# Sums of squares of a two-layer decoder trunk: four column groups of TensorE in place of two, with four-row transposes behind the copies

## The chip, the cores and the metric

The kernel runs on one core of one Trainium2 chip. The metric is the device time of one execution in microseconds (us); lower is better. Three runs of the kernel before gave 801.45, 801.98 and 802.34 us, so its median is 801.98 us.

## The reference

The reference is a decoder trunk of two layers on 528 tokens (16 meta tokens and 512 others) of width 1024. Each layer normalizes its input, projects it, lets a pooling mixer and a latent attention run side by side, and adds their gated merge to the residual stream:

```python
def rmsnorm(x, gain):
    inv = lax.rsqrt(jnp.mean(xf * xf, axis=-1, keepdims=True) + NORM_EPS)
    return xf * inv * gain
...
for l in range(DEPTH):                       # DEPTH = 2
    h = rmsnorm(h_res, norm_gain[l])         # over 1024 features
    proj = h @ w_in[l]                       # u, z, c_q (768), c_kv (256), k_rope, z_mla, gates
    y_pool = (pool_mix(u_pool, ...) * silu(z_pool)) @ pool_w_up[l]
    o_mla = mla(c_q, c_kv, k_rope, ...)      # begins with rmsnorm of c_q and of c_kv
    y_mla = (o_mla * silu(z_mla)) @ mla_w_up[l]
    merged = sigmoid(g_pool) * y_pool + sigmoid(g_mla) * y_mla
    h_res = h_res + merged @ w_out[l]
```

The change concerns two of the norms: that of the layer's input x (a sum of squares over 1024 features per token) and that of c_kv (over 256 features per token).

## The kernel before

Activations are kept transposed: features on the 128 partitions, the 528 tokens along the free axis, so that x is eight tiles of 128 by 528. Every large product is split in three fp32r matmuls (`mm3`, lines 190 to 192: high part of the weights with the high and the low part of the activations, and low part of the weights with the high part). A token axis that is too long for one matmul is done in two segments, `FULL = [(0, 264), (264, 528)]`.

All large products stand in one list (`register`), and `stream()` is a generator that issues them one by one. ScalarE (ACT) converts the weights that arrive by DMA to their high part (line 185), VectorE (DVE) makes the low part (line 186). `go()` issues a layer's other work, and `fill_now(ns)` lets the stream issue about so many nanoseconds of matmuls between two steps of that other work, so that TensorE (PE) has something to do while the other engines work. That is only the order in which the program names the instructions: a scheduler then fixes the order on each engine, after a simulated timeline of its own. Each engine carries out its own instructions strictly in that order, and an instruction that waits holds up all behind it on its engine.

Because the features lie on the partitions, a sum of squares over features is a matmul with a matrix of ones. `norm_sums` (lines 355 to 399) does this once in each layer, for both norms:

1. Eight tiles of squares of x (`xsq`) and two of c_kv (`csq`), each in two segments of 264 tokens, are multiplied by `ones[:, 0:32]` at line 363: 20 matmuls in fp32, each of which the hardware carries out as two passes. A matmul of 32 output rows uses one of four column groups of the array, chosen by `tile_position=(0, r_)`; its result lands in the 32 PSUM partitions of that group. Segment 0 of x uses group 0 and segment 1 uses group 64; c_kv uses groups 32 and 96.
2. Two ACT copies (line 370) bring rows 0 to 63 of `sums` out of PSUM: row 0 holds the sums of x, row 32 those of c_kv. A DVE copy (line 371) repeats the 16 meta tokens eight times in `rep`.
3. Five PE transposes (lines 375 and 376) of 33 rows put the tokens on the partitions, and DVE works out the reciprocal roots (lines 381 to 383, `newton`, lines 391 to 393).
4. `rows` (lines 404 to 410) transposes the roots back into rows of `kinv`, and `spread` (lines 283 to 287) multiplies them by a selector so that every partition holds them: four matmuls at line 286, each followed by an ACT copy at line 287 to `rinv` (for x) or to a tile for c_kv. `ev_u` (line 491) and later evacuations multiply by these.

The other lines that the prediction names: line 346 to 351 make the split input and its squares, line 539 to 550 evacuate the c_q products (ACT copy, DVE remainder, ACT square, GpSimd sum), line 430 is a matmul for k_rope in eight 32-column pieces that uses all four column groups, and line 813 is the 128 by 128 transpose of attention.

PSUM tiles named mm come from a ring of four banks (`mmt`). A PE instruction that needs a bank waits until the last reader of that bank's previous tile has finished.

Of the kernel before, what the change touches and what calls it, by code (L numbers as in the profile page):

```python
# [9 lines left out]
F32 = mybir.dt.float32  # L10
# [3 lines left out]
AF = mybir.ActivationFunctionType  # L14
ALU = mybir.AluOpType
# [3 lines left out]
P = 128  # L19
DEPTH = 2  # L20
D = 1024
SEQ = 512
NM = 16
T = SEQ + NM
HALF = T // 2
# [46 lines left out]
def trunk(ctx, tc, xT, pos, win, wkr, wqb, wkb, wvb, wgr, wpu, wmu, wout, gains, const, yT):  # L72
    nc = tc.nc
    pe, act, dve, gp, sp = nc.tensor, nc.scalar, nc.vector, nc.gpsimd, nc.sync
# [5 lines left out]
    sm = ctx.enter_context(tc.tile_pool(name="sm", bufs=1))  # L80
# [5 lines left out]
    def nm(s):  # L86
        uid[0] += 1
        return f"{s}_{uid[0]}"

    def slot(tag, dt=F32, bufs=1, w=W):  # L90
        return sl.tile([P, w], dt, tag=tag, name=nm(tag), bufs=bufs)

    def tmp(w=W):
        return tp.tile([P, w], F32, tag="tmp", name=nm("tmp"), bufs=3)
# [4 lines left out]
    def mmt():  # L99
        return pp.tile([P, 512], F32, tag="mm", name=nm("mm"), bufs=4)  # L100

    def sct():
        return pp.tile([P, 512], F32, tag="S", name=nm("S"), bufs=3)
# [27 lines left out]
    ident = cst[:, C_ID:C_ID + P]  # L131
    ones = cp.tile([P, P], F32, name="ones")
# [141 lines left out]
    def fill_now(ns):  # L274
        end = clk[0] + ns
        while clk[0] < end and step():
            pass
# [5 lines left out]
    def spread(dst, i):  # L283
        for a, b in FULL:
            ps = mmt()[:, :b - a]
            pe.matmul(ps, sel[0:34, i:i + 1].to_broadcast([34, P]), kinv[:, a:b], start=True, stop=True)
            act.activation(dst[:, a:b], ps, AF.Copy)

    def behind(ins, other):
        tc.add_manual_dep(ins.ins, other.ins.name,  # L290
                          mybir.DependencyInfo(mybir.DependencyClass.Sync, mybir.DependencyReason.DATA))

    def newton(y, a, t):
        dve.tensor_single_scalar(y.bitcast(I32), a.bitcast(I32), 1, op=ALU.logical_shift_right)
        dve.tensor_scalar(y.bitcast(I32), y.bitcast(I32), -1.0, float(0x5F3759DF), op0=ALU.mult, op1=ALU.add)
        dve.tensor_scalar(a, a, -0.5, None, op0=ALU.mult)
        for _ in range(3):
            dve.tensor_mul(t, y, y)
            dve.tensor_mul(t, t, a)
            dve.scalar_tensor_tensor(out=y, in0=t, scalar=1.5, in1=y, op0=ALU.add, op1=ALU.mult)  # L300
# [20 lines left out]
    class Layer:  # L321
# [32 lines left out]

        def norm_sums(self):
            fill_now(2600)
            ps = [mmt(), mmt()]
            for t, r, start, stop in [(self.xsq[k], 0, k == 0, k == 7) for k in range(6)] + [
                    (self.csq[0], 32, True, False), (self.xsq[6], 0, False, False),
                    (self.xsq[7], 0, False, True), (self.csq[1], 32, False, True)]:  # L360
                for s, (a, b) in enumerate(FULL):
                    r_ = r + 64 * s
                    mm = pe.matmul(ps[s][r_:r_ + 32, :HALF], ones[:, 0:32], t[:, a:b], start=start, stop=stop,  # L363
                                   tile_position=(0, r_))
                    if t is not self.csq[1]:
                        behind(mm, self.csq_last)
            sums = tmp()
            rep = sm.tile([64, 8, NM], F32, tag="rep", name=nm("rep"))
            for s, (a, b) in enumerate(FULL):
                act.activation(sums[0:64, a:b], ps[s][64 * s:64 * s + 64, :HALF], AF.Copy)  # L370
            dve.tensor_copy(rep, sums[0:64, 0:NM].unsqueeze(1).to_broadcast([64, 8, NM]))
            fill_now(2600)
            ps = mmt()[:, 0:165].rearrange("p (j c) -> p j c", c=33)
            for j in range(4):
                pe.transpose(ps[:, j, :], sums[0:33, NM + P * j:NM + P * (j + 1)], ident[0:33, 0:33])
            pe.transpose(ps[:, 4, :], rep[0:33].rearrange("p a b -> p (a b)"), ident[0:33, 0:33])
            na = sm.tile([P, 2, 5], F32, tag="na2", name=nm("na2"))
            nt = sm.tile([P, 2, 5], F32, tag="nt2", name=nm("nt2"))
            self.ninv = ny = sm.tile([P, 2, 5], F32, tag="ny2", name=nm("ny2"))
            self.eps = sm.tile([P, 5], F32, tag="eps", name=nm("eps"))  # L380
            dve.tensor_scalar(na[:, 0, :], ps[:, :, 0], 1.0 / D, EPS, op0=ALU.mult, op1=ALU.add)
            dve.tensor_scalar(self.eps, na[:, 0, :], EPS, None, op0=ALU.mult)
            dve.scalar_tensor_tensor(out=na[:, 1, :], in0=ps[:, :, 32], scalar=1.0 / 256, in1=self.eps,
                                     op0=ALU.mult, op1=ALU.add)
            newton(ny, na, nt)
            w = tmp()
            gp.memset(w[:, 0:170], 0.0)
            v = w[:, 0:170].rearrange("p (j c) -> p j c", c=34)
            nv = ny.rearrange("p a j -> p j a")
            nh = sm.tile([P, 5, 2], F32R, tag="nh", name=nm("nh"))  # L390
            dve.tensor_copy(nh, nv)
            dve.tensor_copy(v[:, :, 0:33:32], nh.bitcast(F32))
            dve.tensor_sub(v[:, :, 1:34:32], nv, nh.bitcast(F32))
            fill_now(8200)
            self.rows(v, 34, kinv)
            self.inv, self.cinv = slot("rinv"), slot("cq9")
            fill_now(1300)
            spread(self.inv, 0)
            spread(self.cinv, 1)
            self.st = [sct(), sct()]  # L400
# [727 lines left out]
```

## Time and profile before

| | us |
|---|---|
| median of three runs | 801.98 |
| the profiled execution, its own time | 802.28 |
| its span, from the first to the last instruction | 800.5 |
| PE busy within the span | 792.9 |
| DVE busy | 527.4 |
| ACT busy | 416.9 |
| GpSimd (POOL) busy | 196.4 |
| median duration of one pass at line 363 | 0.386 |
| median duration of one copy at line 370 | 0.386 |

Times within the span are counted from its first instruction. Rows of the timeline give the start, the duration (of several merged rows, from the first start to the last end), the engine, the line, and in brackets how long the engine sat idle before it and what ended that. Matmuls are pipelined: rows overlap, and what a matmul costs is the distance from its start to the next start. PE counts each pass of an fp32 matmul as a row, so line 363 shows 40 rows for each layer.

### The profile page before, as it was taken

To read this page: it belongs to the slowest core of one execution; us is meant where nothing else is said; L and a number is where in the kernel's file an instruction comes from. 1 tells how busy PE (TensorE), PEld (TensorE's weight loads), DVE (VectorE), ACT (ScalarE), POOL (GpSimd) and SP (SyncE) were. 2 spreads that over 40 slices of the span, in tenths; PEclk is the share of its full clock that TensorE was granted. 3 is DMA by queue.
4 is the path that set the end of the run, shared out by engine and by line. 5 is a ranking of instruction groups with operands and counts; after the bars stand their busy time and mean duration, and the time that the engine had idled before them with its cause. 6 is when DMAs were issued, how large, how long until landed. Compare 5 with 4: busy or idle time off the path is not lost.

```text
span 800.5 us, 14638 instructions
## 1 busy us (share of the span) xinstructions
PE 792.9 (99%) x5339; PEld 714.0 (89%) x5339; DVE 527.4 (66%) x1140; ACT 416.9 (52%) x947; POOL 196.4 (25%) x266
## 2 busy tenths in 40 slices
PE   9999999999999999999999999999999999999998
PEld 8889999999999999999997997877788888887887
DVE  5568767437679887585354686665467889665942
ACT  7455645545556665543254456446455666654421
POOL 1024404103333322142000163022024333410600
PEclk9999999999999999999999999999999999999999
DMA  6223233424222222234642222334253322222372
GB/s 240 74 69 93 71 100 90 110 83 143 83 87 87 80 67 67 81 91 142 181 143 73 73 87 86 92 86 119 82 154 97 100 77 79 76 69 78 92 232 97
DMA packets 48872, 80.71 MB, mean 101 GB/s; under 512 B 5904, under 2 KB 14480, under 8 KB 48800
## 3 DMA queue, kind: packets, MB, share of 16 engines
q1 hardware_dynamic: 48656, 79.52, 33.5%
q8 instruction: 42, 0.69, 0.4%
q14 instruction: 30, 0.25, 0.1%
q10 hardware_dynamic: 144, 0.26, 0.1%
HBM read 73.40 MB, written 4.23 MB: 97 GB/s over the span
## 4 chain that ended last, share of the span: by engine, by line
PE 96%; DMA 2%; DVE 1%; ACT 1%; issue 0%; POOL 0%; POOLq 0%
PE mm L190 28%; PE mm L192 28%; PE mm L191 27%; PE mm L813 2%; PE S L191 2%; PE S L192 1%; PE S L190 1%; PE o L819 1%; PE o L818 1%; PE mm L363 1%; PE S L472 1%; DMA xb<-xT 1%; DMA bc<-kdr 1%; PE mm L430 0%; DMA rinv<-win 0%; PE mm L406 0%
## 5 line engine op out<-in xcount | busy, mean ns | idle before, releaser
L190 PE MATMUL mm<-hh,whi 128*128 128x264 f32 (+2 forms) x1096 | 346.0, 318 | 0.4 <-ACT racc L827 0.2
L191 PE MATMUL mm<-hl,whi 128*128 128x264 f32 (+2 forms) x1096 | 343.5, 314 | 0.0
L192 PE MATMUL mm<-hh,wlo 128*128 128x264 f32 (+2 forms) x1096 | 342.0, 315 | 0.0
L186 DVE TENSOR_TENSOR wlo<-raw,whi 128x512 fp32r<-128x512 f32 (+2 forms) x251 | 185.5, 743 | 118.1 <-ACT whi L185 110.8
L185 ACT ACTIVATE whi<-raw 128x512 fp32r<-128x512 f32 (+2 forms) x251 | 150.3, 602 | 186.2 <-PE mm L191 131.1
L190 PEld LDWEIGHTS mm<-hh,whi 128*128 128x128 f32 x1096 | 205.6, 188 | 13.8 <-ACT racc L827 0.5
L191 PEld LDWEIGHTS mm<-hl,whi 128*128 128x128 f32 x1096 | 206.2, 188 | 12.2 <-issue 0.4
L192 PEld LDWEIGHTS mm<-hh,wlo 128*128 128x128 f32 x1096 | 205.0, 188 | 12.7 <-issue 0.4
L719 POOL TENSOR_TENSOR tmp<-kp,bc 64x528 f32<-64x528 f32 x16 | 24.5, 1532 | 113.2 <-DMA bc<-kdr 77.9
L550 POOL TENSOR_TENSOR racc<-racc,tmp 128x264 f32<-128x264 f32 (+1 forms) x15 | 14.1, 942 | 143.1 <-ACT tmp L549 143.0
L791 POOL TENSOR_TENSOR pm<-pa,rs 128x16 f32<-128x16 f32 x32 | 11.6, 361 | 145.6 <-DVE rs L786 145.6
L901 POOL TENSOR_TENSOR tmp<-tmp,xb 128x264 f32<-128x264 f32 (+1 forms) x24 | 26.9, 1143 | 58.6 <-DVE tmp L899 33.0
L747 DVE CUSTOM_DVE_ANT_0 S<-S,maskw,nqs 128x272 f32<-128x272 f32 (+4 forms) x80 | 38.4, 498 | 1.6 <-PE S L192 1.2
L754 ACT ACTIVATE cq<-S,bia 128x400 f32<-128x400 f32 (+2 forms) x48 | 24.6, 516 | 21.5 <-DVE bia L781 11.9
L190 PE MATMUL mm<-u,whi 128*128 128x264 f32 (+1 forms) x108 | 35.3, 327 | 0.0
L192 PE MATMUL mm<-cq,wlo 128*128 128x264 f32 (+1 forms) x108 | 34.8, 323 | 0.0
L192 PE MATMUL mm<-u,wlo 128*128 128x264 f32 (+1 forms) x108 | 34.8, 322 | 0.0
L191 PE MATMUL mm<-cq,whi 128*128 128x264 f32 (+1 forms) x108 | 34.8, 322 | 0.0
L190 PE MATMUL mm<-cq,whi 128*128 128x264 f32 (+1 forms) x108 | 34.7, 322 | 0.0
L281 DVE TENSOR_TENSOR tl<-mm,th 128x512 fp32r<-128x512 f32 (+1 forms) x64 | 29.3, 482 | 6.8 <-ACT th L280 5.8
L793 POOL TENSOR_TENSOR cq<-cq,rs 128x384 f32<-128x384 f32 (+1 forms) x32 | 32.7, 1021 | 0.0
L280 ACT ACTIVATE th<-mm 128x512 fp32r<-128x512 f32 (+1 forms) x64 | 25.4, 433 | 10.7 <-PE mm L813 10.4
(262 smaller groups left out, 1383.6 us busy)
## 6 DMA issues: line engine op xcount, KB each, us to landing
raw<-win SPq DMA_DIRECT2D x143, 256.0 KB, 2.6
raw<-wout SPq DMA_DIRECT2D x32, 256.0 KB, 3.0
bc<-kdr SPq DMA_DIRECT2D x16, 264.0 KB, 3.7
raw<-wpu SPq DMA_DIRECT2D x16, 256.0 KB, 2.6
raw<-wmu SPq DMA_DIRECT2D x16, 256.0 KB, 2.7
raw<-wqb SPq DMA_DIRECT2D x12, 256.0 KB, 2.8
tmp<-xT SPq DMA_DIRECT2D x16, 132.0 KB, 3.0
tmp<-scr SPq DMA_DIRECT2D x7, 256.0 KB, 4.3
```

The costliest lines, as they stand in the source:

```text
L185: act.activation(hi[:, :n], raw[:, :n], AF.Copy)
L186: dve.tensor_sub(lo[:, :n], raw[:, :n], hi[:, :n].bitcast(F32))
L190: pe.matmul(out, wh, xh, start=start, stop=False)
L191: pe.matmul(out, wh, xl, start=False, stop=False)
L192: pe.matmul(out, wl, xh, start=False, stop=stop)
L280: act.activation(hi[:, a:b], src, AF.Copy)
L281: dve.tensor_sub(lo[:, a:b], src, hi[:, a:b].bitcast(F32))
L719: gp.tensor_mul(kf[r0:r0 + 64, :], self.kp[r0:r0 + 64, :], bc[r0:r0 + 64, :])
L747: dve.tensor_tensor_reduce(out=sv, in0=sv, in1=mask, scale=nqs[:, i, h:h + 1], scalar=3e38, op0=ALU.add, op1=ALU.min, accum_out=bia[:, c:c ...
L754: act.activation(pv, sv, AF.Exp, scale=-1.0, bias=bia[:, i:i + 1], accum_out=rs[:, c:c + 1])
L793: gp.tensor_mul(pt[i][:, NM:], pt[i][:, NM:], rs[:, i:i + 1].to_broadcast([P, n - NM]))
L901: gp.tensor_add(t[:, :b - a], t[:, :b - a], self.am[m][:, a:b])
```

## The change

Line 363's matmuls are dealt out differently. One PSUM tile, `px`, takes all sums of x: even tiles of squares in groups 0 (segment 0) and 64 (segment 1), odd ones in groups 32 and 96. A second tile, `pc`, takes the sums of c_kv in the same four groups, one tile of squares for each pair. The matmuls are named in an order in which four successive ones use four different groups. So each sum comes out in two halves that DVE must add.

Four ACT copies, in place of two, fill rows 0 to 127 of `sums`. The five transposes take 97 rows in place of 33, so that rows 0, 32, 64 and 96 (two halves of x, two of c_kv) become four columns. The first four of them get a dependency on the last copy named. DVE has two more small instructions. In the built program the scheduler's order also differs around this work, in both layers; outside of it the order on every engine is the same.

```diff
             fill_now(2600)
-            ps = [mmt(), mmt()]
-            for t, r, start, stop in [(self.xsq[k], 0, k == 0, k == 7) for k in range(6)] + [
-                    (self.csq[0], 32, True, False), (self.xsq[6], 0, False, False),
-                    (self.xsq[7], 0, False, True), (self.csq[1], 32, False, True)]:
+            px, pc = mmt(), mmt()
+            runs = [(px, self.xsq[k], k, k < 2, k >= 6) for k in range(8)] + [(pc, self.csq[m], m, True, True) for m in range(2)]
+            for k in range(0, 10, 2):
                 for s, (a, b) in enumerate(FULL):
-                    r_ = r + 64 * s
-                    mm = pe.matmul(ps[s][r_:r_ + 32, :HALF], ones[:, 0:32], t[:, a:b], start=start, stop=stop,
-                                   tile_position=(0, r_))
+                    for ps, t, m, start, stop in runs[k:k + 2]:
+                        g = 64 * s + 32 * (m % 2)
+                        mm = pe.matmul(ps[g:g + 32, :HALF], ones[:, 0:32], t[:, a:b], start=start, stop=stop,
+                                       tile_position=(0, g))
...
-            rep = sm.tile([64, 8, NM], F32, tag="rep", name=nm("rep"))
+            rep = sm.tile([P, 8, NM], F32, tag="rep", name=nm("rep"))
             for s, (a, b) in enumerate(FULL):
-                act.activation(sums[0:64, a:b], ps[s][64 * s:64 * s + 64, :HALF], AF.Copy)
-            dve.tensor_copy(rep, sums[0:64, 0:NM].unsqueeze(1).to_broadcast([64, 8, NM]))
+                for g, ps in ((0, px), (64, pc)):
+                    copied = act.activation(sums[g:g + 64, a:b], ps[64 * s:64 * s + 64, :HALF], AF.Copy)
+            dve.tensor_copy(rep, sums[:, 0:NM].unsqueeze(1).to_broadcast([P, 8, NM]))
             fill_now(2600)
-            ps = mmt()[:, 0:165].rearrange("p (j c) -> p j c", c=33)
+            ps = mmt()[:, 0:485].rearrange("p (j c) -> p j c", c=97)
             for j in range(4):
-                pe.transpose(ps[:, j, :], sums[0:33, NM + P * j:NM + P * (j + 1)], ident[0:33, 0:33])
-            pe.transpose(ps[:, 4, :], rep[0:33].rearrange("p a b -> p (a b)"), ident[0:33, 0:33])
+                behind(pe.transpose(ps[:, j, :], sums[0:97, NM + P * j:NM + P * (j + 1)], ident[0:97, 0:97]), copied)
+            pe.transpose(ps[:, 4, :], rep[0:97].rearrange("p a b -> p (a b)"), ident[0:97, 0:97])
...
+            dve.scalar_tensor_tensor(out=na[:, 0, :], in0=ps[:, :, 32], scalar=1.0 / D, in1=na[:, 0, :],
+                                     op0=ALU.mult, op1=ALU.add)
             dve.tensor_scalar(self.eps, na[:, 0, :], EPS, None, op0=ALU.mult)
-            dve.scalar_tensor_tensor(out=na[:, 1, :], in0=ps[:, :, 32], scalar=1.0 / 256, in1=self.eps,
-                                     op0=ALU.mult, op1=ALU.add)
+            for c in (64, 96):
+                dve.scalar_tensor_tensor(out=na[:, 1, :], in0=ps[:, :, c], scalar=1.0 / 256,
+                                         in1=self.eps if c == 64 else na[:, 1, :], op0=ALU.mult, op1=ALU.add)
```

## The prediction

> **What bounds the kernel.** I read the page first: busy times, then the chain that ended last.
>
> ```profile
> PE 792.9 (99%) x5339; PEld 714.0 (89%) x5339; DVE 527.4 (66%) x1140; ACT 416.9 (52%) x947; POOL 196.4 (25%) x266
> PE 96%; DMA 2%; DVE 1%; ACT 1%; issue 0%; POOL 0%; POOLq 0%
> ```
>
> The kernel is one long queue on PE. An edit is worth what it takes off PE's own stream, or adds to it in waits; work on ACT and DVE counts only where PE waits for it. So I read PE's timeline around the sums in both layers. Layer 0:
>
> ```profile
> 24.57 1.97 PE L363 MATMUL mm<-cq,ones 128*32 128x264 f32 x16
> 26.37 1.95 PE L363 MATMUL mm<-q,ones 128*32 128x264 f32 x24
> 28.82 0.25 PE L375 MATMUL mm<-cst,tmp 33*128 33x33 f32 x1 [0.50 <-ACT tmp L370]
> 29.23 0.28 PE L191 MATMUL mm<-hl,whi 128*128 128x264 f32 x1
> ...
> 31.29 0.28 PE L190 MATMUL mm<-hh,whi 128*128 128x264 f32 x1
> 31.50 0.37 PE L375 MATMUL mm<-cst,tmp 33*128 33x33 f32 x3
> 31.87 0.39 PE L191 MATMUL mm<-hl,whi 128*128 128x264 f32 x1
> 32.09 0.28 PE L192 MATMUL mm<-hh,wlo 128*128 128x264 f32 x1
> ```
>
> The first transpose stands right behind the sums, so PE waits there for a copy; the other four come 2.7 us later and break the stream again (31.29 to 32.09 is 0.80 for two steps that take 0.24 elsewhere: 0.56 lost). ACT's timeline beside it, with the two copies as one row:
>
> ```profile
> 26.44 0.39 ACT L546 ACTIVATE racc<-mm 128x264 f32<-128x264 f32 x1 [0.56 <-DVE cq L540]
> 28.39 0.80 ACT L370 ACTIVATE tmp<-mm 64x264 f32<-64x264 f32 x2 [1.55 <-PE mm L363]
> 32.70 0.63 ACT L185 ACTIVATE whi<-raw 128x512 fp32r<-128x512 f32 x1 [3.52 <-issue]
> ```
>
> In layer 1 (timeline) 21 matmuls lie between the sums (end 432.7) and the transposes (437.75): the copies are hidden, nothing waits. The chain in order of time gives the prices:
>
> ```profile
> 56.95 1.92 PE mm L430 x32
> ...
> 429.07 3.68 PE mm L363 x40
> ```
>
> **The sums, line 363.** Of the 40 passes in 3.68 us, the busiest column group carries 16 (eight tiles, two passes each). Line 430 deals 32 passes over all four groups, eight to a group, in 1.92. From 16r + e = 3.68 and 8r + e = 1.92: a round costs r = 0.22 and the entry e = 0.16. The change leaves five tiles, ten rounds, to each group: 2.36, so 1.32 less per layer.
>
> **The copies.** Four in place of two, on ACT. The two took 0.80, so one starts 0.41 after the other; the nearest quicker rows are the copies at line 287, which start 0.27 apart. Layer 1: hidden as before. Layer 0: in the built order four transposes still stand right behind the sums and now wait for the last of four copies. The tile of x is complete after round eight, at 24.57 + 7 x 0.22 + 0.39 = 26.5; ACT is free at 26.44 + 0.39 = 26.83. Copies start at 26.83, 27.24, 27.65 and 28.06, the last ends at 28.45 and the transposes start at 28.50 (before: copy end 28.77, transpose 28.82). PE has nothing from about 27.0 to 28.5. So of the 1.32 only 0.32 arrives here; at 0.27 apart it would be 0.74. Behind the copies on ACT is the conversion at 32.70, which waits for a matmul anyway (idle 3.52): the added 0.8 costs nothing; without that cover it would delay the weights of c_q by 0.8.
>
> The Trainium skill has a rule against this change: "TensorEngine Tiling (Array Packing)", section "PSUM Bottleneck", says that tiling speeds up the matmuls but not the copies out of PSUM, which may then bind. Taken for both layers it would leave about 0.3 of each 1.32 and a total near 0.5. The rows agree for layer 0 and not for layer 1, where matmuls cover the copies.
>
> **The transposes.** 33 columns cost about 0.06 each (line 375, layer 1: five from 437.75 in steps of 0.06), 128 columns 0.11 (line 813 in the chain: seven from 203.18 in 0.77). For 97 I take 0.085, in proportion to 128, between these ends; five are 0.42. The 33-row ones also cost at entry and exit: in layer 1, L192 at 437.42 to the second matmul behind, L191 at 438.51, is 1.09 for two steps of 0.23: 0.63 lost. Line 813's use all 128 rows, enter and leave at the ordinary step, and I count 97 rows as they do. Layer 1: 0.63 - 0.42 = 0.21 less. Layer 0: before, L191 starts at 29.23 and 0.56 is lost later, 29.79; after, 28.50 + 0.42 + 0.12 for the step behind = 29.04. So layer 0 gains 0.75, copies and transposes together. With the ends 0.06 and 0.11 the sum of both layers moves by +0.25 and -0.25.
>
> **DVE.** Two more instructions of 128x5 at 0.2 apart, 0.4 per layer, on the way to `rows`. In layer 0 the last (line 393) starts at 37.83 and `rows` at 40.34, with PE not waiting; the built order puts `rows` ten matmuls (1.2) sooner, but the transposes end 2 us sooner. Hidden; without that slack 0.4. In layer 1 four matmuls more lie between, but a GpSimd sum that holds DVE for 1.3 (line 298 at 441.85) may fall into the chain: 0 to 0.3, taken as 0.
>
> **The reordered tail.** `spread` needs four PSUM banks in turn. Layer 0 before, PE, and layer 1 before, PE and ACT:
>
> ```profile
> 42.09 0.63 PE L286 MATMUL mm<-kinv,sel 34*128 34x264 f32 x3
> 43.20 0.38 PE L286 MATMUL mm<-kinv,sel 34*128 34x264 f32 x1 [0.48 <-ACT rinv L287]
> ...
> 450.28 0.51 PE L286 MATMUL mm<-kinv,sel 34*128 34x264 f32 x2
> ...
> 451.76 0.51 PE L286 MATMUL mm<-kinv,sel 34*128 34x264 f32 x2
> ```
> ```profile
> 450.70 0.67 ACT L287 ACTIVATE rinv<-mm 128x264 f32<-128x264 f32 x2 [0.36 <-PE mm L286]
> 451.80 0.63 ACT L185 ACTIVATE whi<-raw 128x512 fp32r<-128x512 f32 x1 [0.43 <-ACT rinv L287]
> ```
>
> In layer 1 seven matmuls part the two pairs, and a bank is free again when the second pair comes. In the built order of the changed kernel the seven stand ahead, the four at line 286 follow each other, and two of the four banks hold products that wait for `rinv`. So the third waits for the copy of the first, the fourth for that of the second, and the next product for that of the third. ACT has the conversion of line 185, which waits for the matmul two before line 286, ahead of these copies. From the first L286 as 0: conversion 0.04, first copy 0.57 (0.54 behind it, as 451.80 to the next L287), its end 0.96, third L286 1.02, its end 1.40, copy 1.44 to 1.82, next product 1.87, the step behind 2.09. From the last L192 at -0.21 that is 2.30, less two steps of 0.12: 2.06 lost. Before, each pair lost 0.64 (450.06 to 450.94 and 451.55 to 452.43, 0.88 for 0.24): 1.28. So 0.78 is given back; if the copies fell clear of the conversion it would be about 0.5, and 0 if the order hid it. Layer 0 keeps its four in a row, with 0.03 more wait.
>
> **Sum.** Layer 0: 0.75 - 0.03 = 0.72. Layer 1: 1.32 + 0.21 - 0.78 = 0.75. Together 1.47 less: 802.28 becomes 800.81. The profiled run lies 0.3 above the median 801.98, so beside that median 800.5. About 0.2%, or 1.6 us, is what a measurement of this kernel can tell from no change; the forecast lies at that edge.
>
> **Rivals.** *Cheaper copies* (0.15): ACT starts them 0.27 apart in layer 0; gain 1.9, 800.1. For: line 287. Against: the two at line 370 did not. *The tail costs nothing* (0.10): the four at line 286 meet free copies; gain 2.25, 799.7. For: the 0.5 of slack above. Against: the bank order, as in layer 0's row with 0.48. *Clock* (0.08): slower. PE's longest idle in this trace is 0.50, and the granted clock stays 1.00; the new wait is 1.5. The start shows what a slow clock costs: from the first matmul at 1.05 to about 5.7 matmuls take twice their time (two of L190 at 4.96 take 0.99, at 7.56 0.41). Should PE slow down after an idle between 0.5 and 1.5, a stretch of 4.6 at half speed costs 2.3: 802.8, and 805.1 if it lasts twice as long. The Trainium skill, "TensorE: Matmul & The Clock Gate", Part 1, puts the idle window at about 3.4 us; by that nothing happens, and no run here shows it. *No concurrency* (0.05): four groups writing one PSUM tile take turns, line 363 stays at 3.68. Layer 0's four copies then run from 28.39 to 30.0 and its second step ends at 30.6 against 29.79, 0.8 slower; layer 1 keeps 0.21 - 0.78, 0.6 slower: 803.4. Against: line 430 does just this.
>
> **Numbers.** The forecast has 0.62, its own range a gain of 0.9 to 2.0 (transposes 0.25 either way, layer 1's tail and DVE 0.3); a bit under half of that passes 1.6, so 0.29 faster and 0.33 same. The first two rivals are faster (0.25); the last two split between same (0.07) and slower (0.06). That makes 0.54, 0.40, 0.06. The range 799.2 to 801.7 takes in the forecast with its unknown costs, the two better cases and 0.3 for the spread of the medians.
>
> **What would show it.** Line 363 with 40 rows in about 2.4 in both layers; in layer 0 the transposes near 28.5 with an idle of 1.5 put down to ACT; in layer 1 two waits at line 286 or behind, together about 0.8 more than before; rows of line 190 still 0.12 apart behind layer 0's wait. A line 363 of 3.7, or matmuls 0.24 apart after 28.5, would prove the forecast wrong; so would new waits in attention, where the order is unchanged.

## The result, and the profile after

The changed kernel takes 800.28 us (median of 18 runs, 799.41 to 801.61), the kernel before 801.93 us on the same chip (18 runs, 800.57 to 803.01). The medians lie 1.65 us apart. The ratio over all runs is 0.9982, 95% interval 0.9975 to 0.9989: 1.4 us less, 0.9 to 2.0. The forecast was 800.5 and a gain of 1.47. At 0.18% the gain lies just under the 0.2% that the prediction took as the least that can be told from no change, but the interval does not reach a ratio of 1, so the gain is clear of the noise even so.

The profiled execution of the changed kernel has a span of 798.5 us, against 800.5. Its page, busy times and the chain that ended last:

```profile
PE 789.6 (99%) x5339; PEld 712.5 (89%) x5339; DVE 527.6 (66%) x1144; ACT 418.6 (52%) x951; POOL 196.5 (25%) x266
PE 94%; DVE 1%; ACT 1%; DMA 0%; issue 0%; ACTq 0%
```

PE is busy 3.3 us less (792.9 before), with as many passes, while the span shrank by 2.0. The other 1.3 has turned into idle time. PE's timeline in layer 0 shows the largest new wait:

```profile
24.59 1.10 PE L363 MATMUL mm<-cq,ones 128*32 128x264 f32 x16
25.51 1.52 PE L363 MATMUL mm<-q,ones 128*32 128x264 f32 x24
28.41 0.55 PE L376 MATMUL mm<-cst,tmp 97*128 97x97 f32 x4 [1.38 <-ACT tmp L371]
28.74 0.37 PE L190 MATMUL mm<-hh,whi 128*128 128x264 f32 x1
...
29.20 0.25 PE L377 MATMUL mm<-cst,rep 97*128 97x97 f32 x1
29.23 0.37 PE L190 MATMUL mm<-hh,whi 128*128 128x264 f32 x1
```

The sums now end near 27.0, but the transposes (now line 376) wait until 28.41 for the fourth copy, 1.38 idle where there was 0.50. ACT's timeline has the four copies as one row:

```profile
26.48 0.39 ACT L550 ACTIVATE racc<-mm 128x264 f32<-128x264 f32 x1 [0.56 <-DVE cq L544]
26.76 1.59 ACT L371 ACTIVATE tmp<-mm 64x264 f32<-64x264 f32 x4
32.00 0.63 ACT L185 ACTIVATE whi<-raw 128x512 fp32r<-128x512 f32 x1 [3.65 <-issue]
```

Layer 1, PE's timeline: the sums are as short as in layer 0 and nothing waits for the copies, but the third of the four products of line 286 waits for a copy to `rinv`, and the next product behind the four waits for a later copy of line 287:

```profile
427.70 1.10 PE L363 MATMUL mm<-cq,ones 128*32 128x264 f32 x16
428.61 1.52 PE L363 MATMUL mm<-q,ones 128*32 128x264 f32 x24
430.06 0.50 PE L190 MATMUL mm<-hh,whi 128*128 128x512 f32 x1
...
448.32 0.50 PE L286 MATMUL mm<-kinv,sel 34*128 34x264 f32 x2
449.31 0.66 PE L286 MATMUL mm<-kinv,sel 34*128 34x264 f32 x2 [0.50 <-ACT rinv L287]
450.18 0.39 PE L190 MATMUL mm<-kh,whi 128*128 128x264 f32 x1 [0.20 <-ACT cq L287]
450.40 0.28 PE L191 MATMUL mm<-kl,whi 128*128 128x264 f32 x1
```

**Where the time went, by stages.** The stream issues the same 4692 matmuls of lines 190 to 192 in every kernel here, so the start of the n-th in one trace less that of the n-th in another is the time gained up to there. Taken at four points of the trace of before (24.4 us, ahead of the sums of layer 0; 60; 427.5, ahead of those of layer 1; 470), this splits each run into the two stages that the edits touch and the stretch between, where the order on PE is unchanged. All runs of this study, gain over the first trace of before (us, minus is slower); the last columns have nothing to do with the traces, they are the medians of the timed runs, and the gain over the kernel before as it was timed in the same batch (before_again was executed once, with the profiler on, 802.17 us):

| kernel | layer 0 | between | layer 1 | the two layers | median | gain of the medians |
|---|---|---|---|---|---|---|
| the change | 0.72 | 0.61 | 0.70 | 1.42 | 800.28 | 1.65 |
| after_again | 0.70 | 0.36 | 0.71 | 1.41 | 800.10 | 1.33 |
| before_again | -0.03 | 0.91 | 0.00 | -0.03 | | |
| hold_alone | -0.44 | 1.10 | 0.02 | -0.42 | 802.10 | -0.45 |
| no_hold | 1.15 | 0.43 | 0.67 | 1.81 | 799.98 | 1.67 |
| two_groups | -0.08 | 0.69 | -0.21 | -0.29 | 801.92 | -0.27 |
| one_group | -3.25 | -0.53 | -3.37 | -6.62 | 809.00 | -7.57 |
| free_banks | 1.44 | 0.15 | 1.91 | 3.35 | 798.35 | 3.30 |
| late_free | 2.89 | 0.44 | 1.91 | 4.80 | 796.93 | 4.50 |

For the change, the sum of the two layers is 1.42 where the forecast had 1.47, and the sums agree with the gains of the medians within 0.3 in each row but one_group's.

### The profile page after: what moved, and what is told of

The parts are those of the page before. It is cut to its first block, busy times and chain, and to the rows that moved or that the text cites. A ratio compares the mean times of both kernels' runs of the same rounds, so it can differ in the third digit from the quotient of the medians.

```text
span 798.5 us, 14645 instructions
## 1 busy us (share of the span) xinstructions
PE 789.6 (99%) x5339; PEld 712.5 (89%) x5339; DVE 527.6 (66%) x1144; ACT 418.6 (52%) x951; POOL 196.5 (25%) x266
## 4 chain that ended last, share of the span: by engine, by line
PE 94%; DVE 1%; ACT 1%; DMA 0%; issue 0%; ACTq 0%
PE mm L190 28%; PE mm L191 27%; PE mm L192 27%; PE mm L817 2%; PE S L191 1%; PE S L192 1%; PE S L190 1%; PE o L823 1%; PE o L822 1%; PE S L476 1%; PE mm L434 0%; PE mm L410 0%; DMA raw<-wmu 0%; PE mm L363 0%; DVE wlo L186 0%
## 5 line engine op out<-in xcount | busy, mean ns | idle before, releaser
L190 PE MATMUL mm<-hh,whi 128*128 128x264 f32 (+2 forms) x1096 | 346.3, 318 | 0.4 <-ACT whi L185 0.2
L192 PE MATMUL mm<-hh,wlo 128*128 128x264 f32 (+2 forms) x1096 | 342.0, 315 | 0.0
L190 PEld LDWEIGHTS mm<-hh,whi 128*128 128x128 f32 x1096 | 205.6, 188 | 13.7 <-ACT racc L831 0.5
L192 PEld LDWEIGHTS mm<-hh,wlo 128*128 128x128 f32 x1096 | 205.1, 188 | 12.5 <-issue 0.4
L190 PE MATMUL mm<-u,whi 128*128 128x264 f32 (+1 forms) x108 | 35.3, 327 | 0.0
L192 PE MATMUL mm<-cq,wlo 128*128 128x264 f32 (+1 forms) x108 | 34.8, 323 | 0.0
L192 PE MATMUL mm<-u,wlo 128*128 128x264 f32 (+1 forms) x108 | 34.8, 322 | 0.0
L190 PE MATMUL mm<-cq,whi 128*128 128x264 f32 (+1 forms) x108 | 34.6, 322 | 0.0
```

The source lines that it names most:

```text
L190: pe.matmul(out, wh, xh, start=start, stop=False)
L192: pe.matmul(out, wl, xh, start=False, stop=stop)
```

## The experiments

**The traces themselves, a second time.** The first pair of traces differs by 2.0 us of span, the medians by less. Is the 0.6 between the layers part of the change? The changed kernel and the kernel before were each profiled once more, unedited.

> The changed kernel as it is, a second trace. Theory (the gain is 1.4 to 1.5, in the two layers' norm stages; what the first pair of traces showed between them, 0.6, was the luck of the profiled execution of before): from the sums of layer 0 to the first attention 0.7 better than before, from the sums of layer 1 to behind line 286 0.7 better, and the same times there as in the first trace within 0.05, while the stretch between differs by some tenths either way. 800.3 us. Rival (the change moves the transfers in attention for good): the stretch between is again 0.6 better than in every trace of before.

> The kernel before as it is, a second trace. Theory: between the norm stages (attention of layer 0, where the rows of line 176 to 186 wait for a transfer) it differs from the first trace by some tenths, most likely 0.3 to 0.6 faster; the norm stages agree within 0.05. Rival (the change moves the transfers for good): the stretch between agrees with the first trace within 0.1.

Measured: 800.10 us against 801.43 for before (ratio 0.9985, 0.9976 to 0.9994). The two norm stages repeat within 0.03 in both kernels; the stretch between does not. Most of it lies at 174 to 186 us, where the attention of layer 0 waits for a transfer. The profile's list of DMA issues for the window 170 to 195 us has it (name, queue, count, size, median us from issue to landing): the first row is of the first trace of before, the second of its second, the third of the first trace after, the last of one_group.

```profile
bc<-kdr SPq DMA_DIRECT2D x5, 264.0 KB, 4.7
```
```profile
bc<-kdr SPq DMA_DIRECT2D x5, 264.0 KB, 3.7
```
```profile
bc<-kdr SPq DMA_DIRECT2D x5, 264.0 KB, 4.2
```
```profile
bc<-kdr SPq DMA_DIRECT2D x4, 264.0 KB, 5.2
```

Gain from 174 to 186 over the first trace of before, for the last three: 0.75, 0.49 and -0.49. With 3.9 (hold_alone) 0.76 is gained, with 4.0 (two_groups) 0.68, with 4.3 (after_again) 0.35, with 4.4 (no_hold) 0.27, with 4.5 (late_free) 0.24, with 5.0 (free_banks) -0.34. So PE pays for the landing time one to one, and from about 3.9 down it gains no more. At 4.7, the first trace of before had one of the slower ones. The rival falls: the second trace of before is faster in this stretch than either trace of the changed kernel, so 0.6 of the first pair's 2.0 is the luck of single executions.

**The hold alone.** To the kernel before, nothing but this:

```diff
-                act.activation(sums[0:64, a:b], ps[s][64 * s:64 * s + 64, :HALF], AF.Copy)
+                copied = act.activation(sums[0:64, a:b], ps[s][64 * s:64 * s + 64, :HALF], AF.Copy)
...
-                pe.transpose(ps[:, j, :], sums[0:33, NM + P * j:NM + P * (j + 1)], ident[0:33, 0:33])
+                behind(pe.transpose(ps[:, j, :], sums[0:33, NM + P * j:NM + P * (j + 1)], ident[0:33, 0:33]), copied)
```

> The kernel before, with nothing but the dependency of its first four transposes on the second copy. In layer 0 all four stand behind the sums, the fifth three matmuls later; in layer 1 the order stays nearly as before, the two pairs of line 286 are parted by six matmuls. Theory: layer 0 waits 0.42 longer for the second copy, and the broken stream three matmuls later (0.56) shrinks to one transpose with its entry and exit (0.2 to 0.5): zero, within 0.4, 801.9 us. Rival (the hold brings the gain): 800.5 us.

Measured: 802.10 us against 801.65 (ratio 1.0004, 0.9996 to 1.0013). It gains nothing; layer 0 loses 0.44, just past the 0.4 that had been allowed, because the wait grew to 0.91 and the fifth transpose still breaks the stream. PE's timeline of layer 0:

```profile
29.23 0.44 PE L375 MATMUL mm<-cst,tmp 33*128 33x33 f32 x4 [0.91 <-ACT tmp L370]
...
30.16 0.25 PE L376 MATMUL mm<-cst,rep 33*128 33x33 f32 x1
30.34 0.39 PE L190 MATMUL mm<-hh,whi 128*128 128x264 f32 x1
```

**The grouping alone.** The changed kernel with `behind(..., copied)` taken off the transposes:

```diff
-                behind(pe.transpose(ps[:, j, :], sums[0:97, NM + P * j:NM + P * (j + 1)], ident[0:97, 0:97]), copied)
+                pe.transpose(ps[:, j, :], sums[0:97, NM + P * j:NM + P * (j + 1)], ident[0:97, 0:97])
```

> The changed kernel without the dependency of the transposes on the last copy. In the built order of layer 0 one transpose now stands right behind the sums, 19 matmuls of the stream follow, then the other four transposes; five matmuls (twelve before) lie between line 411 and line 286. In layer 1 one matmul parts the first transpose from the rest, the four at line 286 stay in a row. Theory: in layer 0 the first transpose waits for the second copy alone, which ends near 27.65: 0.8 of the idle 1.4 goes; five matmuls (0.6) are too few to hide the copies to kinv, which costs 0.3 to 0.5. 799.9 us, range 799.5 to 800.4: within 0.5 of the change. Rival (the hold is where the gain comes from): the gain of 1.5 over before goes, 801.5 or more.

Measured: 799.98 us (ratio 0.9978, 0.9969 to 0.9987), as forecast and, by the medians, no worse than with the hold. In layer 0 the wait is 0.97 in place of 1.38 (PE's timeline, then ACT's; this trace is 0.86 late already ahead of the sums, before the edit comes into play):

```profile
25.42 1.10 PE L363 MATMUL mm<-cq,ones 128*32 128x264 f32 x16
26.34 1.52 PE L363 MATMUL mm<-q,ones 128*32 128x264 f32 x24
28.82 0.30 PE L376 MATMUL mm<-cst,tmp 97*128 97x97 f32 x1 [0.97 <-ACT tmp L371]
```
```profile
27.59 1.59 ACT L371 ACTIVATE tmp<-mm 64x264 f32<-64x264 f32 x4
```

The time is the one forecast, but by two misses that cancel. Of the wait, 0.8 was to go and only 0.41 went: the four copies start 0.40 apart, so the second ends near 28.4 and the third near 28.8, and the first transpose at 28.82 stands right behind the third, not the second. And the 0.3 to 0.5 that was to be lost again at line 286 did not come: the layer keeps 1.15.

So the gain belongs to the grouping. The hold makes the first transpose wait for one more copy and costs 0.4 in layer 0 (0.72 against 1.15); between the gains of the medians it is 0.0 to 0.3, which is within their scatter.

**Two groups at a time.** Is it concurrency that shortens line 363? Only the order in which the products are named is changed:

```diff
-            for k in range(0, 10, 2):
-                for s, (a, b) in enumerate(FULL):
-                    for ps, t, m, start, stop in runs[k:k + 2]:
+            for k in (0, 2, 4, 6, 1, 3, 5, 7, 8, 9):
+                for s, (a, b) in enumerate(FULL):
+                    ps, t, m, start, stop = runs[k]
```

> The changed kernel with line 363's twenty products named two column groups at a time: first all even tiles of x (groups 0 and 64), then the odd ones (32 and 96), then c_kv. Tiles, copies, transposes, DVE and the order of the rest stay. Theory (concurrency of four groups is the gain of 1.32 per layer): twenty rounds of 0.22 and the entry 0.16, 4.56 us for 40 passes in place of 2.36, so layer 1 loses 2.2. In layer 0 the copies run from about 28.3, the last ends at 30.0 and the transposes start at 30.05 in place of 28.41: 1.6. Together 3.8 slower than the change, 804.1 us, 2.2 slower than before. Rival (the gain comes from the held transposes and the new order, not from the groups): line 363 takes about the same, 800 to 801 us.

Measured: 801.92 us (ratio 1.0004, 0.9995 to 1.0013): the whole gain is gone, but only 1.7 of the expected loss of 3.8 came, by the two layers. Line 363 takes 3.28 in layer 1 (428.20 to 431.48), not 4.56, and in layer 0 the transposes start at 28.98, not 30.05. Line 363 is still 0.40 shorter than before in each layer, and the later copies of layer 0 and the tail of layer 1 take that back. PE's timeline, where cq and q tell the tiles of squares apart (cq: x0 to x3; q: x4 to x7 and c_kv):

```profile
428.20 1.08 PE L363 MATMUL mm<-cq,ones 128*32 128x264 f32 x8
429.11 0.39 PE L363 MATMUL mm<-q,ones 128*32 128x264 f32 x2
429.13 0.42 PE L363 MATMUL mm<-cq,ones 128*32 128x264 f32 x2
...
430.04 1.50 PE L363 MATMUL mm<-q,ones 128*32 128x264 f32 x16
431.48 0.50 PE L190 MATMUL mm<-hh,whi 128*128 128x512 f32 x1
```

The program names x0, x2 (cq), x4, x6 (q) for groups 0 and 64 and only then x1 (cq) for group 32. Yet a pass with cq starts at 429.13, right behind the first pass of x4 at 429.11 and ahead of those of x6. My step "named in pairs, so two at a time" was wrong. I formed another theory from this row: each column group has a queue of its own, one pass running and three waiting, and PE's sequencer stops only at a product whose queue is full. By that the second pair of groups starts four rounds after the first (0.89; measured 0.93) and has ten rounds to go: 14 x 0.22 + 0.16 = 3.24.

**One group after the other** tests that theory with an order that it says is much worse:

```diff
-            for k in range(0, 10, 2):
-                for s, (a, b) in enumerate(FULL):
-                    for ps, t, m, start, stop in runs[k:k + 2]:
+            for k_, s in [(k_, s) for m_ in range(2) for s in range(2) for k_ in (m_, m_ + 2, m_ + 4, m_ + 6, m_ + 8)]:
+                a, b = FULL[s]
+                ps, t, m, start, stop = runs[k_]
```

> The changed kernel with line 363's products named one column group after the other: five to group 0, five to 64, five to 32, five to 96. Theory from two_groups' trace (each group has a queue of its own: a pass that runs and three that wait; PE's sequencer stops at a product whose group's queue is full, and products of other groups behind it stop too): each group's ten passes begin six rounds after those of the group ahead, 28 rounds and the entry, 28 x 0.22 + 0.16 = 6.3 us in place of 2.36. Layer 1 loses 3.9. In layer 0 the last copy waits for the last round: end 31.3, transposes at 31.4 in place of 28.4, 3.0. Together 6.9 over the change, 807.2 us. Rival 1 (no queue, a product runs beside others only if they are neighbours in the program): 37 rounds or more (three neighbours overlap at the borders), 8.3 us, 811 us or more. Rival 2 (any order is as good, the groups run free): 800.3 us.

Measured: 809.0 us (ratio 1.0092, 1.0078 to 1.0105). Line 363 in layer 1, PE's timeline:

```profile
433.05 1.08 PE L363 MATMUL mm<-cq,ones 128*32 128x264 f32 x4
433.97 0.83 PE L363 MATMUL mm<-q,ones 128*32 128x264 f32 x3
434.42 0.41 PE L363 MATMUL mm<-cq,ones 128*32 128x264 f32 x1
434.63 0.39 PE L363 MATMUL mm<-q,ones 128*32 128x264 f32 x1
...
434.86 0.39 PE L363 MATMUL mm<-q,ones 128*32 128x264 f32 x1
...
435.08 0.39 PE L363 MATMUL mm<-q,ones 128*32 128x264 f32 x1
...
435.78 0.41 PE L363 MATMUL mm<-cq,ones 128*32 128x264 f32 x1
...
437.15 0.41 PE L363 MATMUL mm<-cq,ones 128*32 128x264 f32 x1
...
439.49 0.50 PE L190 MATMUL mm<-hh,whi 128*128 128x512 f32 x1
```

The four groups begin at 433.05, 434.42, 435.78 and 437.15: 1.37 apart, six rounds of 0.22 and a little. The whole takes 6.44, expected 6.3; both rivals (8.3, and 2.4) are out. One waiting line of a fixed length for all groups together is out too: when a later group begins, three passes of each earlier group that still works are yet to start, three in all here (434.63, 434.86 and 435.08) and six in two_groups, where two groups work at a time. Against the change, layer 1 lost 4.07 (3.9 expected). Layer 0 lost 3.97, not 3.0: all four copies began only at 30.94 and the transposes stood behind them at 32.63; the expectation had counted one copy behind the last round. The medians show another 0.95 that the stages don't; in the profiled execution, 0.5 is the slow transfer above. Whether the timed runs had it too, and what the rest is, stays open.

**The tail in banks that are free.** In the changed kernel the four products of line 286 take three banks of the scores and one of attention's output, none in use at that time, and are held behind the last copy to `kinv`, which keeps them in a row (the hold is not in the lines shown):

```diff
-    def spread(dst, i):
-        for a, b in FULL:
-            ps = mmt()[:, :b - a]
+    def spread(dst, i, banks):
+        for (a, b), bank in zip(FULL, banks):
+            ps = bank()[:, :b - a]
...
-            spread(self.inv, 0)
-            spread(self.cinv, 1)
+            spread(self.inv, 0, (sct, sct))
+            spread(self.cinv, 1, (sct, ot))
```

> The changed kernel with the four products of line 286 in PSUM banks that nothing uses at that time (three of the scores, one of attention's output) and held behind the last copy to kinv; the four stay in a row, 25 matmuls behind line 411 in both layers. Theory (the tail's 2.06 in layer 1 and the same four in layer 0 are waits for banks): four steps of 0.12 and the entry and exit 0.4 stay, 0.88. Layer 1 gains 2.06 - 0.88 = 1.2, layer 0, which has one wait of 0.48 and a second behind, about 0.7: 798.4 us, range 798.0 to 799.0. If the later rinv makes u wait, up to 0.5 of this is lost. Rival (the waits of the tail are covered elsewhere, or given back by a later wait): 800.3 us, no change.

Measured: 798.35 us (ratio 0.9955, 0.9941 to 0.9968). Layer 1 gains 1.21 and layer 0 0.72 more than with the change alone, 1.2 and 0.7 having been expected. PE's timeline in layer 1 (line 286 is now 289):

```profile
447.48 0.28 PE L190 MATMUL mm<-kh,whi 128*128 128x264 f32 x1
447.69 0.63 PE L289 MATMUL S<-kinv,sel 34*128 34x264 f32 x3
448.16 0.28 PE L289 MATMUL o<-kinv,sel 34*128 34x264 f32 x1
448.37 0.39 PE L191 MATMUL mm<-kl,whi 128*128 128x264 f32 x1
448.60 0.28 PE L192 MATMUL mm<-kh,wlo 128*128 128x264 f32 x1
```

From L190 to L192 is 1.12 for two steps of 0.12: 0.88 lost, as worked out, against 2.06. The rival is refuted: the waits at line 286 were on the path, and nothing later takes their place.

**And the transposes moved away from the sums.** The same, with more of the stream between the sums and the transposes of layer 0:

```diff
-            fill_now(2600)
+            fill_now(3900 if self.l == 0 else 2600)
             ps = mmt()[:, 0:485].rearrange("p (j c) -> p j c", c=97)
...
-            fill_now(8200)
+            fill_now(6900 if self.l == 0 else 8200)
```

> The changed kernel with the four products of line 286 in free banks as in free_banks and, in layer 0, the stream filled for 3900 in place of 2600 ns between the sums and the transposes (and for 6900 in place of 8200 before rows): in the built order 24 matmuls of the stream stand between the sums and all five transposes, 72 between these and rows, 28 between line 411 and line 286. Theory: the 24 matmuls (2.9 us) cover the copies, so layer 0's wait of 1.4 goes and nothing takes its place: 798.35 - 1.4 = 797.0 us, range 796.6 to 797.5; the stage of layer 0 gains 2.8 over before (free_banks 1.44). Rival (rinv comes 15 matmuls later in the order, so u waits for it, or DVE's chain makes rows wait): part or all of the 1.4 comes back, 797.5 to 798.4.

Measured: 796.93 us (ratio 0.9941, 0.9928 to 0.9953), 4.7 us under before and 3.2 under the changed kernel run beside it. This is the best kernel of the study. PE's timeline in layer 0 (lines shifted by four):

```profile
29.89 0.28 PE L192 MATMUL mm<-hh,wlo 128*128 128x264 f32 x1
30.00 0.50 PE L380 MATMUL mm<-cst,tmp 97*128 97x97 f32 x4
30.34 0.25 PE L381 MATMUL mm<-cst,rep 97*128 97x97 f32 x1
30.37 0.37 PE L190 MATMUL mm<-hh,whi 128*128 128x264 f32 x1
```

No bracket: the transposes wait for nothing, and the next product starts 0.37 after the first of them. Layer 0 gains 2.89 over before, 2.8 having been expected. The list of PE's waits for 20 to 60 us is empty for this kernel. For the changed kernel it reads (line waited for, us in total, times, longest):

```profile
PE mm L376 <- ACT tmp L371: 1.4, 1, 1.4
PE mm L286 <- ACT rinv L287: 0.5, 1, 0.5
```

## Why the prediction was right

- **The sums.** Predicted 2.36 per layer; 427.70 to 430.06 is 2.36. Rounds are 0.22 apart, and within a round each pass starts 7 ns after the one ahead. That only the busiest group's rounds count holds while successive products go to different groups, as in both kernels; two_groups and one_group show that the order of naming decides it otherwise.
- **The copies of layer 0.** Predicted 26.83 to 28.45 and transposes at 28.50; measured 26.76 to 28.35 and 28.41. The rival *cheaper copies* falls: four copies in 1.59 are 0.40 apart. The Trainium skill's "PSUM Bottleneck" ("TensorEngine Tiling (Array Packing)") describes layer 0 rightly, with its 1.38 idle; in layer 1, where matmuls cover the copies, PE waits for none of them. Behind the copies, the idle time before the conversion of line 185 is put down to "issue", which names no matmul; yet it starts 0.70 sooner than before (32.00 against 32.70), as the products of the stream do there, so taking it to wait for PE was right.
- **The transposes.** Taken as 0.085 each without entry or exit. PE's timelines of layer 1, before and after:

```profile
437.42 0.40 PE L192 MATMUL mm<-hh,wlo 128*128 128x512 f32 x1
437.75 0.43 PE L375 MATMUL mm<-cst,tmp 33*128 33x33 f32 x4
...
438.51 0.40 PE L191 MATMUL mm<-hl,whi 128*128 128x512 f32 x1
```
```profile
435.48 0.40 PE L192 MATMUL mm<-hh,wlo 128*128 128x512 f32 x1
435.71 0.50 PE L376 MATMUL mm<-cst,tmp 97*128 97x97 f32 x4
...
436.39 0.39 PE L191 MATMUL mm<-hl,whi 128*128 128x512 f32 x1
```

The same two steps with the five transposes between take 1.09 before and 0.91 after: 0.18 less, 0.21 predicted. In layer 0 two small misses cancel, which is luck: the transposes begin 0.1 sooner than predicted, and cost 0.1 more, since the fifth stands apart from the other four (29.20, behind three products) and breaks the stream a second time, while the sum had all five in a row.
- **DVE.** The list of PE's waits around both layers has no entry for `rows`: hidden, as taken.
- **The tail.** Predicted from the first L286 as 0: third at 1.02, next product 1.87, the step behind 2.09. Measured 0.99, 1.86, 2.08. The loss of 0.78 is 0.79 by the stream's starts. *The tail costs nothing* is refuted by free_banks too.
- **The clock.** Behind the idle of 1.38 the products are 0.12 apart, as elsewhere; the rival falls for an idle of this length. The granted clock is given as 1.00 there, but so it is for the slow start of the trace before, so the distance is the evidence. By the window of about 3.4 us in "TensorE: Matmul & The Clock Gate" of the Trainium skill, Part 1, nothing happens; the trace agrees. In no trace here does PE idle for longer than 1.38 between two matmuls, so the window itself is not tested.
- **The sum.** 0.72 and 0.75 predicted, 0.72 and 0.70 measured; the 0.72 to the digit is owed in part to the two misses above. By its own bound of 0.2%, the prediction gave 0.54 to a gain above it and 0.40 to one below, and the less likely side came. What the prediction did not foresee is the 0.6 between the layers in the first pair of traces, which before_again showed to be no part of the change. The transfer behind it stood on the chain of before with 4.70 us; the forecast compared medians, in which its scatter averages out, and so did not need it.

The prediction held because its terms were distances between starts in the timelines and not shares of a busy time, and because the two waits that the change itself makes, 1.4 in layer 0 and 0.8 more lost in layer 1, were worked out instruction by instruction from the built order.

## What to carry to other kernels

When PE is the queue that sets the time, a shorter stage pays only if the results leave PSUM behind other matmuls: here 1.32 us were saved in each layer, and 0.9 of it was given back in layer 0 to copies that nothing covered, 0.8 in layer 1 to a ring of four banks; the cheaper transposes, 0.3 and 0.2, brought each layer back to 0.7. Look for the wait that the saving makes before making it; banks that another phase leaves idle, and 24 matmuls between the sums and the transposes that read their copies, brought another 3.2 us on top of the grouping's 1.4. And compare stages by the starts of the same instruction in two traces, since two traces of the kernel before differ by 0.9 in a stretch that the change does not touch.

## What the hardware showed that I had not expected

In these traces the column groups of TensorE act as if each ran from a queue of its own. In one_group the first pass for group 64 starts at 434.42, while three passes for group 0 that the program names earlier start at 434.63, 434.86 and 435.08. A group takes one pass every 0.22 us (two per fp32 product of 264 columns); three more can wait behind it, and a product for a group whose queue is full stops all behind it, so that groups of ten passes named one after the other begin six rounds (1.37) apart. So the strict order of instructions on an engine, as the kernel is described above, is not kept between column groups at line 363. The queues and their depth are inferred from two orders, not read from a counter.

The transfer of 264 KB to `bc` in attention landed after 3.7 to 5.2 us in the ten traces, and above about 3.9 us it moved the products behind it, at 186 us, by as much.
